# Macaron feed-forward layers of a decoder trunk: gate and up sums with the tokens stationary and 512 weight columns moving

## The chip, the cores and the metric

One Trainium2 chip, one of its NeuronCores. The metric is the device time of one execution of the whole program, in microseconds. The kernel before takes 970.08 us, the median of three runs (969.25 to 970.21).

## What is computed

Two layers of a decoder over 256 tokens with 1024 features, all in f32. Each layer is a half-weighted SwiGLU, a token mixer (short convolution and sliding-window attention in layer 0, causal block attention in layer 1), cross-attention to a memory of 256 rows, and a second half-weighted SwiGLU. A last RMSNorm follows. Cut to what the change touches:

```python
def rmsnorm(x, g):
    return x * lax.rsqrt(jnp.mean(x * x, axis=-1, keepdims=True) + EPS) * g

def swiglu(x, w_gate, w_up, w_down):          # 1024 -> 2816 -> 1024
    return (jax.nn.silu(x @ w_gate) * (x @ w_up)) @ w_down

for l in range(2):
    x = x + 0.5 * swiglu(rmsnorm(x, ffn1_norm[l]), ...)
    x = x + mixer(rmsnorm(x, mix_norm[l]))
    x = x + memory_cross_attention(rmsnorm(x, xa_norm[l]), ...)
    x = x + 0.5 * swiglu(rmsnorm(x, ffn2_norm[l]), ...)
return rmsnorm(x, final_norm)
```

So there are four feed-forward blocks (FFNs) in a run, each with 22 x 8 weight tiles of 128 x 128 for the gate, as many for up, and as many for down.

## The kernel before

**Layout.** The stream `x` lies with features on the partitions: 8 tiles (KT) of 128 features x 256 tokens. A matmul therefore has a weight tile as the stationary operand (loaded by LDWEIGHTS) and the tokens as the moving one, and its output has the output features on the partitions. The 22 (FT) hidden tiles `h[f]` come out in the layout that the down product needs.

**Precision.** Each f32 operand is split in two fp32r parts, hi and lo, and a product is hi*hi + hi*lo + lo*hi. `mm` (L389) does it with two matmuls for one weight tile: w-hi against 512 columns (x-hi and x-lo side by side, L392) and w-lo against the 256 of x-hi (L393). The bank then holds two halves, which `join` (L401) adds: a ScalarE copy (L402) and a VectorE add (L403). `mm_narrow` (L395) does it with three matmuls of 256 columns (L397 to L399) into one half. `group_tok` (L437, used by `v_group` in layer 1) is the third form: tokens stationary, four weight tiles (512 columns) moving, three matmuls for each half of the tokens (L449 to L451).

**Weights.** `Stream` reads all weights from DRAM in the order of use: chunks of 16 tiles (1 MB) through SP's queue, four `raw` buffers. A block is 8 tiles; ScalarE makes its hi part (L127) and VectorE its lo part (L128), into five `whi`/`wlo` buffers. `take` (L155) asks for the tile or the four tiles of a step and has blocks up to four ahead split; `fill` and `flush` write the splits that are due into the program at the places where they are called. The very first 32 tiles come with x in eight smaller loads of their own (`load_first`).

**Norm.** The gain goes into the tiles of x (`normed_tile`, L313). 1/rms of a token is left out and multiplied in later. `norm_scale` (L341) makes it: sums over features turned on TensorE (L353, or L355 for the first FFN), `rcol` on GpSimd (L360; a value for each token on the partitions), and with `wide` it is spread on TensorE (L366) and copied (L368) to `rbc`, where it lies along the free axis.

**An FFN** (`ffn`, L497). `gate_up` (L512) makes one f tile of gate or up: eight `mm`, then `join`. `evac` (L530) then multiplies the gate by `rbc` (L532), takes silu (L533), multiplies by up (L535) and splits into `h[f]` (L465, L466). The first FFN starts with `gates` (L501): the first four gate tiles together, in the order in which the first loads land. `down` (L540) makes one of the eight output tiles from all 22 `h`; its sum is joined, scaled by 0.5 and `rbc` (L549) and added to x (`add_to_x`, L459), and the next norm's tile is made at once. The last FFN ends in `down_tok` (L555), with tokens on the output partitions; there `to_tokens` (L482) turns x with VectorE's 32 x 32 transposes (L489) and DMAs through DRAM (L492, L494).

**Order.** `Order.run` writes fillers (matmul parts with their cost) and timed tasks out in one program order; the tile framework then orders each engine's instructions by its own simulated timeline, apart from those that are pinned. Each engine runs its list in order. PSUM has 4 banks `acc`, 2 `sc`, 2 `tr`.

## Time and profile before

| what | us |
|---|---|
| median of three runs | 970.08 (969.25 to 970.21) |
| span of the profiled execution, first to last instruction | 966.6 |
| gate and up of the FFN that begins at 312.68 (352 tiles) | 115.72 |
| down of the FFN that begins at 428.40 (176 tiles) | 57.80 |
| VectorE and ScalarE busy in that gate and up stage | 96.31 and 75.59 |
| VectorE and ScalarE busy in that down stage | 41.64 and 31.48 |

The times of the runs and the profile are of separate executions. The profiled one has no time of its own beside its span; what lies around the span is about 3.5 us if it ran like the median (970.08 less 966.6). The stage rows come from the view of the profile that sums busy time by stretch. Durations of matmuls overlap, since they are pipelined: what one costs is the distance from its start to the next one's start, which the view in order of time shows.

### The profile page before, as it was taken

How to read it: one execution, taken by the hardware profiler on the slowest of the kernel's cores; microseconds unless marked ns; L12 is line 12 of the kernel's file. 1: busy time of each engine (PE TensorE's matmuls, PEld its weight loads, DVE VectorE, ACT ScalarE, POOL GpSimd, SP SyncE). 2: the span in 40 equal slices, each digit the busy share in tenths (PEclk: the TensorE clock that was granted, in tenths of full speed). 3: DMA queues.
4: the chain of work that ended last, by engine and by line, in shares of the span. 5: the costliest groups of instructions: out<-in, count | busy, mean ns of one | idle time of the engine just before them, and what ended most of it. 6: DMA issues, size and time to landing. Idle time of an engine off the chain costs nothing.

```text
span 966.6 us, 17028 instructions
## 1 busy us (share of the span) xinstructions
PE 958.3 (99%) x6606; PEld 902.1 (93%) x6606; DVE 757.1 (78%) x1350; ACT 614.4 (64%) x1144; POOL 56.0 (6%) x95
## 2 busy tenths in 40 slices
PE   9999999999999999999999999999999999999997
PEld 9999999999999999999999999999999999999896
DVE  6979767898878888876778778677878789878663
ACT  7767655697658766665556666556786677666541
POOL 0410000001000000000000000000000003400011
PEclk9999999999999999999999999999999999999999
DMA  9797556455535655656556565565645356775531
GB/s 371 284 342 269 199 193 217 168 187 201 186 133 208 228 187 206 208 189 213 194 199 204 194 213 188 204 208 184 222 144 192 120 175 239 240 259 183 212 131 44
DMA packets 29922, 196.74 MB, mean 204 GB/s; under 512 B 3848, under 2 KB 4872, under 8 KB 7184
## 3 DMA queue, kind: packets, MB, share of 16 engines
q1 hardware_dynamic: 27072, 187.44, 55.0%
q0 software_dynamic: 2192, 7.37, 2.2%
q8 instruction: 52, 0.85, 0.3%
q10 hardware_dynamic: 576, 0.83, 0.2%
q14 instruction: 30, 0.25, 0.1%
HBM read 193.51 MB, written 5.27 MB: 206 GB/s over the span
## 4 chain that ended last, share of the span: by engine, by line
PE 99%; DMA 0%; DVE 0%; POOLq 0%; ACT 0%; SPq 0%; issue 0%; DVEq 0%
PE acc L392 41%; PE acc L393 20%; PE acc L397 8%; PE acc L399 8%; PE acc L398 8%; PE acc L581 1%; PE acc L580 1%; PE acc L579 1%; PE acc L923 1%; PE acc L922 1%; PE acc L921 1%; PE sc L579 0%; PE sc L581 0%; PE sc L580 0%; DMA raw<-in_w 0%; PE tr L756 0%
## 5 line engine op out<-in xcount | busy, mean ns | idle before, releaser
L127 ACT ACTIVATE whi<-raw 128x1024 fp32r<-128x1024 f32 (+2 forms) x377 | 369.5, 986 | 269.7 <-PE acc L392 131.9
L128 DVE TENSOR_TENSOR wlo<-raw,whi 128x1024 fp32r<-128x1024 f32 (+2 forms) x377 | 427.0, 1136 | 143.4 <-ACT whi L127 140.2
L392 PE MATMUL acc<-x,whi 128*128 128x512 f32 x1344 | 441.3, 383 | 0.0
L393 PE MATMUL acc<-x,wlo 128*128 128x256 f32 x1344 | 365.5, 273 | 0.0
L392 PEld LDWEIGHTS acc<-x,whi 128*128 128x128 f32 x1344 | 253.7, 189 | 34.8
L393 PEld LDWEIGHTS acc<-x,wlo 128*128 128x128 f32 x1344 | 258.0, 192 | 0.3
L392 PE MATMUL acc<-h,whi 128*128 128x512 f32 x462 | 151.3, 382 | 0.0
L393 PE MATMUL acc<-h,wlo 128*128 128x256 f32 x462 | 125.4, 273 | 0.0
L392 PEld LDWEIGHTS acc<-h,whi 128*128 128x128 f32 x462 | 87.1, 189 | 12.1
L397 PE MATMUL acc<-x,whi 128*128 128x256 f32 x352 | 95.5, 279 | 1.4 <-ACT whi L127 1.4
L399 PE MATMUL acc<-x,wlo 128*128 128x256 f32 x352 | 95.9, 278 | 0.0
L398 PE MATMUL acc<-x,whi 128*128 128x256 f32 x352 | 95.7, 277 | 0.0
L393 PEld LDWEIGHTS acc<-h,wlo 128*128 128x128 f32 x462 | 88.7, 192 | 0.2
L399 PE MATMUL acc<-h,wlo 128*128 128x256 f32 x322 | 87.7, 275 | 0.0
L398 PE MATMUL acc<-h,whi 128*128 128x256 f32 x322 | 87.7, 275 | 0.0
L397 PE MATMUL acc<-h,whi 128*128 128x256 f32 x322 | 86.5, 277 | 0.0
L403 DVE TENSOR_TENSOR w<-acc,w 128x256 f32<-128x256 f32 x189 | 78.7, 417 | 3.8 <-ACT w L402 3.5
L402 ACT ACTIVATE w<-acc 128x256 f32<-128x256 f32 x189 | 69.9, 370 | 8.3 <-PE acc L393 8.3
L397 PEld LDWEIGHTS acc<-x,whi 128*128 128x128 f32 x352 | 66.4, 192 | 1.8 <-ACT whi L127 1.6
L398 PEld LDWEIGHTS acc<-x,whi 128*128 128x128 f32 x352 | 66.8, 192 | 0.2
L399 PEld LDWEIGHTS acc<-x,wlo 128*128 128x128 f32 x352 | 66.7, 192 | 0.2
L398 PEld LDWEIGHTS acc<-h,whi 128*128 128x128 f32 x322 | 61.7, 192 | 0.1
(213 smaller groups left out, 1192.2 us busy)
## 6 DMA issues: line engine op xcount, KB each, us to landing
raw<-in_w SPq DMA_DIRECT2D x171, 1024.0 KB, 4.9
dists<-line POOLq DMA_DIRECT2D x2, 1536.0 KB, 13.3
raw<-in_memT SPq DMA_DIRECT2D x3, 1024.0 KB, 4.9
raw<-in_w SPq DMA_DIRECT2D x6, 384.0 KB, 6.8
bias<-dists POOLq DMA_DIRECT2D x2, 1024.0 KB, 11.1
x<-in_xT SPq DMA_DIRECT2D x1, 1024.0 KB, 7.5
tok<-q POOLq DMA_DIRECT2D x32, 32.0 KB, 3.5
bias<-tok POOLq DMA_DIRECT2D x1, 1024.0 KB, 8.1
```

The lines of the kernel that those rows point to most:

```text
L127: for ins in (self.nc.scalar.activation(hi[:, at], src, AF.Copy), self.nc.vector.tensor_tensor(lo[:, at], src, hi[:, at].bitcast(F32), op= ...
L128: self.nc.vector.tensor_tensor(lo[:, at], src, hi[:, at].bitcast(F32), op=ALU.subtract)):
L392: nc.tensor.matmul(ps, w[0], x2.both, start=start, stop=False)
L393: nc.tensor.matmul(ps[:, :S], w[1], x2.high, start=False, stop=stop)
L397: nc.tensor.matmul(ps[:, :S], w[0], x2.high, start=start, stop=False)
L398: nc.tensor.matmul(ps[:, :S], w[0], x2.low, start=False, stop=False)
L399: nc.tensor.matmul(ps[:, :S], w[1], x2.high, start=False, stop=stop)
L402: nc.scalar.activation(halves(out), unpaired(ps[:, S:]), AF.Copy)
L403: nc.vector.tensor_tensor(halves(out), unpaired(ps[:, :S]), halves(out), op=ALU.add)
L579: nc.tensor.matmul(ps, hh, wh, start=f == 0, stop=False)
L580: nc.tensor.matmul(ps, hh, wl, start=False, stop=False)
L581: nc.tensor.matmul(ps, hl, wh, start=False, stop=f == FT - 1)
```

## The change

Gate and up are computed with the tokens stationary. `rows_of` makes a row group: for each of the 8 feature tiles k it takes four weight tiles at once and runs, for each half u of the tokens, three matmuls with 512 weight columns moving into that half's bank; four f tiles of gate, then the same four of up. The last two f tiles (22 = 5 x 4 + 2) share one group of two gate and two up tiles (`both`). There is no sum of halves to join, and since tokens now lie on the partitions of the bank, 1/rms is a factor for each partition: ScalarE takes silu straight from the bank with `rcol` as its scale, and VectorE multiplies the up bank by `rcol` and by that result. `h` so made has tokens on the partitions; `turned_back` brings it into the layout that down needs, with VectorE's 32 x 32 transposes, one DMA to DRAM and four back, and the split into hi and lo reads what came back. Groups of four tiles use GpSimd's DMA queue, the last two tiles ScalarE's; two buffers (`v`, `k2`) take turns. `down` adds both halves of its bank to x, each with the factor 0.5. `downs` writes the first two output tiles with the first 20 `h`, then both with the last two, then the other six. `gates`, `evac`, `gate_up` and, in the FFNs, the spread 1/rms are gone; `make_bias` is told to wait for `rcol` instead of `rbc`.

```diff
--- before.py
+++ after.py
@@ -152,7 +152,7 @@
         while self.due or self.part:
             self.fill()
-    def take(self, name, layer, row, col, n=1, rows=1):
+    def take(self, name, layer, row, col, n=1, rows=1, other=None):
@@ -160,6 +160,7 @@
         for k in range(n):
             at = k % 2 * P
             self.order.append((name, layer, row, col + k * P, 1) if n == 1 else
+                              ((name, other)[k // 2], layer, row, col + at, 1) if other else
                               (name, layer, row, col + 2 * at + k // 2, 2) if rows == 1 else
                               (name, layer, row + at, col + k // 2, 2))
         b, o = divmod(i, BLK)
@@ -496,69 +497,111 @@
     def ffn(which, layer, n, nxt, first=False, last=False):
         h = [None] * FT
-        cur = {}
-
-        def gates():
...
+        gate, up = f"{which}_w_gate", f"{which}_w_up"
+        def turned_back(f0, s, c):
+            t = act.tile([P, 8 * c * 32], F32, name=("v", "k2")[f0 // 4 % 2], bufs=1)
+            to = t.rearrange("p (b u c i) -> p u c b i", b=4, u=2, c=c)
+            for u in range(2):
+                nc.vector.transpose(to[:, u], s[u].rearrange("p (c b j) -> p c b j", c=c, b=4))
+            queue = nc.gpsimd if c == 4 else nc.scalar
+            d = dram.tile([P, 8 * c * 32], F32, name="turn", bufs=2)
+            queue.dma_start(d, t)
+            for b in range(4):
+                queue.dma_start(t[32 * b:32 * b + 32].rearrange("j (a x) -> j a x", a=4),
+                                d.rearrange("(a j) (b x) -> b j a x", a=4, b=4)[b])
+            back = t.rearrange("p (a u c i) -> p c u a i", a=4, u=2, c=c)
+            for i in range(c):
+                h[f0 + i] = x2 = h_tile()
+                hi, lo = (m.rearrange("p u (a i) -> p u a i", a=4) for m in (x2.hi, x2.lo))
+                nc.scalar.activation(hi, back[:, i], AF.Copy)
+                nc.vector.tensor_tensor(lo, back[:, i], hi.bitcast(F32), op=ALU.subtract)
+        def rows_of(name, c, bank, evac, other=None):
+            ps = []
+            def part(ks):
+                def go():
+                    if ks[0] == 0:
+                        ps.extend(bank() for _ in range(2))
+                    for k in ks:
+                        wh, wl = (paired(w) for w in ws.take(name, layer, k * P, c, 4, other=other))
+                        for u in range(2):
+                            xh, xl = (n.x[k].v[:, u, m] for m in range(2))
+                            nc.tensor.matmul(ps[u], xh, wh, start=k == 0, stop=False)
+                            nc.tensor.matmul(ps[u], xh, wl, start=False, stop=False)
+                            nc.tensor.matmul(ps[u], xl, wh, start=False, stop=k == KT - 1)
+                    ws.flush()
+                    if ks[-1] == KT - 1:
+                        when_scaled(n, lambda: evac(ps))
+                return always, go, len(ks) * 1300
+            return [part(range(k, k + 2)) for k in range(0, KT, 2)]
+        def hidden(f0):
+            state = {}
+            def r(u):
+                return n.rcol[:, u:u + 1]
+            def gated(ps):
+                state["s"] = [w2() for _ in range(2)]
+                for u in range(2):
+                    nc.scalar.activation(state["s"][u], ps[u], AF.Silu, scale=r(u))
+            def product(ps):
+                for u, t in enumerate(state["s"]):
+                    nc.vector.scalar_tensor_tensor(t, ps[u], r(u), t, op0=ALU.mult, op1=ALU.mult)
+                turned_back(f0, state["s"], 4)
+            def both(ps):
+                ts = [w2()[:, :S] for _ in range(2)]
+                for u, t in enumerate(ts):
+                    g, v = ps[u].rearrange("p (a b) -> p b a", b=2)[:, 0], ps[u].rearrange("p (a b) -> p b a", b=2)[:, 1]
+                    nc.scalar.activation(t, g, AF.Silu, scale=r(u))
+                    nc.vector.scalar_tensor_tensor(t, v, r(u), t, op0=ALU.mult, op1=ALU.mult)
+                turned_back(f0, ts, 2)
+            if f0 + 4 > FT:
+                return rows_of(gate, f0 * P, acc_tile, both, up)
+            return (rows_of(gate, f0 * P, sc_tile if f0 // 4 % 2 else acc_tile, gated) +
+                    rows_of(up, f0 * P, acc_tile, product))
+        def down(j, ks, cell):
             def go():
                 if ks[0] == 0:
...
+                    cell.append(acc_tile())
+                ps = cell[0]
+                ws.fine = j == KT - 1
                 for k in ks:
...
                     w = ws.take(f"{which}_w_down", layer, k * P, j * P)
                     (mm_narrow if ws.fine else mm)(ps, w, h[k], k == 0, k == FT - 1)
...
+                if ks[-1] == FT - 1:
+                    for part in (ps[:, :S],) if ws.fine else (ps[:, :S], ps[:, S:]):
+                        nc.vector.scalar_tensor_tensor(halves(x[:, j]), unpaired(part), 0.5, halves(x[:, j]),
+                                                       op0=ALU.mult, op1=ALU.add)
+                    normed_tile(nxt, j, x[:, j], x)
                 ws.flush()
...
+            return always, go, len(ks) * 327
+        def downs():
+            cells = [[] for _ in range(KT)]
+            early = range(FT // 4 * 4)
+            late = range(FT // 4 * 4, FT)
+            return ([down(j, early, cells[j]) for j in range(2)] + [down(j, late, cells[j]) for j in range(2)] +
+                    [down(j, range(FT), cells[j]) for j in range(2, KT)])
         def down_tok():
             late = 2 * (ws.BUFS - 1)
-            half_r = act.tile([P, 2], F32, name="half_r", bufs=1)
-            pe.after(30000, lambda: nc.vector.tensor_scalar(half_r, n.rcol, 0.5, None, op0=ALU.mult), 0)
             pss, got, mean = {}, {}, [EPS, EPS]
             def part(fs, *regions):
@@ -587,7 +630,7 @@
             def evac_tok(u, at, ps):
                 y = xtok[:, u, at]
-                nc.vector.scalar_tensor_tensor(y, ps, half_r[:, u:u + 1], y, op0=ALU.mult, op1=ALU.add)
+                nc.vector.scalar_tensor_tensor(y, ps, 0.5, y, op0=ALU.mult, op1=ALU.add)
                 ms = act.tile([P, 1], F32, name="mean", bufs=4)
                 junk = w2()[:, :at.stop - at.start]
                 nc.vector.tensor_tensor_reduce(junk, y, y, 1.0 / D, mean[u], ALU.mult, ALU.add, ms)
@@ -614,18 +657,15 @@
         if first:
             for k in range(KT):
                 pe.after(12000 + 1800 * (k // 2), lambda k=k: squares(n, k, x), 0)
-        norm_scale(n, 18900 if first else 2300, unpin=True, turn=not first)
...
+        norm_scale(n, 18900 if first else 2300, unpin=True, turn=not first, wide=False)
         if last:
             xtok = act.tile([P, 2, D], F32, name="bias", bufs=1)
             gfin = act.tile([P, D], F32, name="kT", bufs=1)
             src = a["final_norm"]
             nc.sync.dma_start(gfin, bass.AP(tensor=src.tensor, offset=src.offset, ap=[[0, P], [1, D]]))
             when_scaled(n, lambda: pe.after(6000, lambda: to_tokens(xtok), 0))
...
+        ups = [f for f0 in range(0, FT, 4) for f in hidden(f0)]
+        pe.run(ups + (down_tok() if last else downs()))
     def small(name):
@@ -1104,7 +1144,7 @@
     def biases():
         nc.vector.tensor_scalar(nsinks, vecs[:, VCOL["sinks"]:VCOL["sinks"] + 8], -1.0, None, op0=ALU.mult)
-        make_bias(n.rbc)
+        make_bias(n.rcol)
         early["bias"] = load_bias(0)
     mn = new_normed("mem_norm", "h", FT, keep=True)
```

More of the change, by code (lines that the diff above doesn't have):

```diff
@@ L513, in go @@
+        def down(j, ks, cell):
             def go():
                 if ks[0] == 0:
-                    cur[f, part] = acc_tile()
-                ps = cur[f, part]
-                w = f"{which}_w_{'up' if part else 'gate'}"
-                narrow = first and f < SIDE
+                    cell.append(acc_tile())
+                ps = cell[0]
+                ws.fine = j == KT - 1
                 for k in ks:
-                    (mm_narrow if narrow else mm)(ps, ws.take(w, layer, k * P, f * P), n.x[k], k == 0, k == KT - 1)
@@ L616, in ffn @@
                 pe.after(12000 + 1800 * (k // 2), lambda k=k: squares(n, k, x), 0)
-        norm_scale(n, 18900 if first else 2300, unpin=True, turn=not first)
-        parts = (range(4), range(4, KT))
-        ups = [(always, gates, FIRST * 327)] if first else []
-        ups += [gate_up(f, part, ks) for f in range(FT) for part in range(2) for ks in parts
-                if not (first and part == 0 and f < SIDE)]
+        norm_scale(n, 18900 if first else 2300, unpin=True, turn=not first, wide=False)
         if last:
@@ L627, in ffn @@
             when_scaled(n, lambda: pe.after(6000, lambda: to_tokens(xtok), 0))
-        pe.run(ups + (down_tok() if last else [down(j) for j in range(KT)]))
+        ups = [f for f0 in range(0, FT, 4) for f in hidden(f0)]
+        pe.run(ups + (down_tok() if last else downs()))
     def small(name):
```

34 lines of the change are left out of this document (removed).

## The prediction

> **What bounds the kernel now.** I read the page first: span, busy shares, slices, the chain that ended last.
>
> ```profile
> span 966.6 us, 17028 instructions
> PE 958.3 (99%) x6606; PEld 902.1 (93%) x6606; DVE 757.1 (78%) x1350; ACT 614.4 (64%) x1144; POOL 56.0 (6%) x95
> PEclk9999999999999999999999999999999999999999
> PE 99%; DMA 0%; DVE 0%; POOLq 0%; ACT 0%; SPq 0%; issue 0%; DVEq 0%
> ```
>
> The reader is to see one engine in charge. TensorE (PE) is 99% of the chain, and its granted clock is full in all slices. VectorE's 78% and ScalarE's 64% lie beside it. So two things alone move the end: the time that a matmul takes until the next can start, and any new place where PE waits. Busy time can't tell the first, since matmuls overlap; the view in order of time can. First the pair that `mm` issues for one weight tile, in a gate and up stage:
>
> ```profile
> 379.93 0.38 PE L392 MATMUL acc<-x,whi 128*128 128x512 f32 x1
> ...
> 400.89 0.38 PE L392 MATMUL acc<-x,whi 128*128 128x512 f32 x1
> ```
>
> From the first row to the last lie 64 pairs without a gap: 20.96 us / 64 = 327.5 ns for a tile. Now whole stages, in the view of busy time by stretch (stretch, sum, then busy time and instructions of PE, PEld, DVE, ACT, POOL, then clock, DMA share, GB/s). The second row is `v_group` of layer 1, the form that the change brings:
>
> ```profile
> 312.68:428.40 115.72, 115.72 (x711) 106.53 (x709) 96.31 (x163) 75.59 (x139) 1.61 (x1) 1.00 0.59 208
> 670.88:681.23 10.35, 10.35 (x50) 9.08 (x49) 10.08 (x19) 8.68 (x17) 0.00 (x0) 1.00 0.64 222
> 5.98:27.97 21.99, 21.99 (x195) 21.95 (x196) 18.48 (x29) 18.84 (x34) 1.30 (x2) 1.00 1.02 416
> ```
>
> `v_group` is 8 steps of k with 6 matmuls: 48 in 10.35 us (the count has two that reach in), 215.6 ns each, for 32 tiles. That is 323.4 ns a tile. Both forms stream 768 columns for a tile, so the gain can't be large. It is 4.1 ns a tile, because four 512-wide and four 256-wide matmuls become six of 512. VectorE was 97% and ScalarE 84% busy in that stretch, so the step holds beside full neighbours.
>
> Over N columns the Trainium skill ("TensorE: Matmul & The Clock Gate", section Back-to-back issue gap) gives a start-to-start of N / 2.4 + 2.5 ns. By it the wide step is 215.8 ns, and the trace agrees (215.6); but the pair would be 325.0 ns where the trace has 327.5. By the page a tile would gain 1.3 ns, by the rows 4.1, and the measurement decides.
>
> **The change part by part.** Everything is counted against the profiled span of 966.6 us and carried over to the median: 970.08 less 966.6 is 3.5 us around the span, which no part of the change touches.
>
> *Three full FFNs.* Now 115.72 us. After: 352 x 323.4 ns = 113.84. Two of the four small transposes stay, those of the sums. Those of the spread 1/rms go:
>
> ```profile
> L366 PE MATMUL tr<-ident,rcol x12: 272/272/273, 30.6 to 803.2; 128*128 128x128 f32 x12
> ```
>
> 115.72 less 352 x 327.5 ns (115.28) leaves 0.44 us for four, 0.11 each. So 113.84 + 0.22 = 114.06, a gain of 1.66 us each, 5.0 in three.
>
> *The first FFN.* 288 of its tiles run as pairs: 288 x 4.1 ns = 1.18, plus the spread 0.22, makes 1.4 us. Its first 64 run with three 256-wide matmuls and take 21.99 us from 5.98 on (third row above). About 0.4 of that is the four short matmuls of the sums, which stay; 64 x 323.4 ns + 0.4 = 21.1, a gain of 0.9. Against it stands the start:
>
> ```profile
> 5.41 0.52 ACT L127 ACTIVATE whi<-raw 128x384 fp32r<-128x384 f32 x1 [1.41 <-DMA raw<-in_w]
> 5.96 0.56 DVE L128 TENSOR_TENSOR wlo<-raw,whi 128x384 fp32r<-128x384 f32 x1 [1.45 <-ACT whi L127]
> 5.98 0.38 PE L397 MATMUL acc<-x,whi 128*128 128x256 f32 x1 [1.43 <-ACT whi L127]
> ```
>
> A wide matmul needs all four tiles, so it can't start before 5.98 (one narrow matmul did), and its lo part is there at 6.52. Between nothing and 0.32 us is lost there; with the early matmul I take 0.3. First FFN together: 1.4 + 0.9 - 0.3 = 2.0 us.
>
> *Down, `down_tok`, attention, end.* Same matmuls. The two halves of a bank are now added by two VectorE instructions in place of join, scale and add; PE waits for none of these today. I count nothing.
>
> **PE gains 5.0 + 2.0 = 7.0 us**, if nothing new makes it wait.
>
> *Load on the other engines.* For four f tiles VectorE had 8 joins (417 ns), 4 + 4 multiplies (417, 424) and 4 lo parts (415); ScalarE 8 copies (370), 4 silus (408), 4 hi parts (406). After: VectorE two 512-wide multiplies from the bank, two transposes, 4 lo parts; ScalarE two 512-wide silus and 4 hi parts.
>
> ```profile
> L403 DVE TENSOR_TENSOR w<-acc,w 128x256 f32<-128x256 f32 x189 | 78.7, 417 | 3.8 <-ACT w L402 3.5
> L402 ACT ACTIVATE w<-acc 128x256 f32<-128x256 f32 x189 | 69.9, 370 | 8.3 <-PE acc L393 8.3
> L535 DVE TENSOR_TENSOR w<-w,w 128x256 f32<-128x256 f32 x88 | 36.7, 424 | 8.3 <-DVE w L403 0.9 <-ACT w L533 0.8
> L465 ACT ACTIVATE h<-w 128x256 fp32r<-128x256 f32 x96 | 38.1, 406 | 2.2 <-DVE w L535 1.0 <-DVE w L887 1.0
> L466 DVE TENSOR_TENSOR h<-w,h 128x256 fp32r<-128x256 f32 x96 | 39.2, 415 | 0.0
> L489 DVE STREAM_TRANSPOSE q<-x 128x512 f32<-128x512 f32 x4 | 2.7, 695 | 0.0
> 955.21 0.75 DVE L590 SCALAR_TENSOR_TENSOR bias<-sc,half_r,bias 128x512 f32<-128x512 f32 x1 [5.50 <-PE sc L581]
> ```
>
> VectorE falls from 8.4 to 2 x 0.75 + 2 x 0.70 + 1.7 = 4.6 us for 20.7 us of PE, ScalarE from 6.2 to about 3. It frees time, but not time on the path.
>
> *The way of h through DRAM is the one new wait that can reach PE.* Its places are the first `h` of the fifth group (f 16 to 19) and f 20, 21. Earlier groups have 40 us and more until down begins; the last FFN's `down_tok` uses one f in 1.3 us, so f 16 has 31 us. Rows for the transfers, of the DMA view and of GpSimd's order of time:
>
> ```profile
> raw<-in_w SPq DMA_DIRECT2D x171, 1024.0 KB, 4.9
> tok<-q POOLq DMA_DIRECT2D x32, 32.0 KB, 3.5
> bias<-tok POOLq DMA_DIRECT2D x1, 1024.0 KB, 8.1
> out<-bias ACTq DMA_DIRECT2D x2, 192.0 KB, 2.1
> L492 POOL DMA_DIRECT2D tok<-q x32: 582/582/624, 813.9 to 839.9; - x32
> 50.52 1.09 POOL L869 DMA_DIRECT2D dists<-line  x2 [3.64 <-DMA line<-kT]
> DMA to landing us min/median/max: 1.8/3.5/5.4
> ```
>
> *Cover of f 16*: the last row group, 48 x 0.2156 = 10.35 us, and 16 tiles of down, 16 x 0.3275 = 5.24: 15.6 us. *Chain*: two multiplies and two transposes, 2.9, with part of a weight split ahead 3.5; the round trip R; then ScalarE's hi part, VectorE's lo part and parts of two splits, 1.9. It is in time for R up to 10.2. R is a 512 KB write, three more issues (0.58 each, 1.75) and the landing of the last 128 KB read. From below two landings at 1.8 (the shortest of the 32): 5.4. From above two at 8.1 (1 MB on this queue): 17.95. I take 4.9 for the write and 3.5 for the read, the rows nearest in size and queue: 10.15. So f 16 is just in time, and f 17 to 19 follow at 0.41 us against 0.33 needed. **0.3 us lost in each of three FFNs, 1.0 us together.** From below it is nothing, from above 7.8 each.
>
> *Cover of f 20*: 40 tiles of down, 13.1 us. Chain: 2.2 of arithmetic, a 256 KB write on ScalarE's queue (2.1 for 192 KB; 2.5), the reads 3.5, 1.9 at the end: 10.1. In time, but ScalarE issues these DMAs itself: each read waits for the write in ScalarE's own list, and behind it stand hi parts of weights and of f 16 to 19. PE has four blocks (10.5 us) of split weights ahead, so 3 us of that cost nothing.
>
> By the Trainium skill ("DMA: Bandwidth & Descriptors", section Anatomy of one DMA) a transfer through GpSimd's queue costs 2.0 us plus its bytes at 436 GB/s, an estimate of 3.2 us for the write and 2.3 for a read. Then R would be 7.3 and nothing would be late. The trace speaks against it: 32 KB took 3.5 us in the median, and PE gains 7.0 instead of 6.0.
>
> **Sum**: 970.08 - 7.0 + 1.0 = **964.1 us**.
>
> **The rivals.**
>
> *Late turns that take back the gain.* PE waits in the first output tile of down. If R is 12.0 to 13.1, 1.8 to 2.9 us are lost in each of three FFNs, 5.1 to 8.7, and the kernel ends within 0.2% of before. For: another kind of transfer on this queue took 8.1. Against: weight loads of 1 MB land in 4.9 beside the same traffic.
>
> *Late turns that make it slower.* The same place, with R over 13.1: PE stands 2.9 us or more in each of three downs. At R = 15 it is 4.8 each, 14.4 together: 977.5 us. Above 13.1 ScalarE is also held at the hi parts of f 16, the turn of f 20 starts late, and a second wait follows. For: all five DMAs of a group wait in GpSimd's list one after another, and a 24 KB write alone held it 3.64 us. Against: GpSimd is idle in these stretches.
>
> *The wide form doesn't run at 215.6 in an FFN.* If the 4.1 ns came from traffic in the stage and not from the alternation of widths, only the spread (4 x 0.22) and part of the first tiles remain, about 1.5 us, less 1.0 for the turns: 969.6. Against: `v_group` had VectorE at 97%. Halfway, with a pair that an undisturbed stage would run 2.5 ns faster than 327.5, a tile gains 1.6 ns and the run ends at 970.08 - (1344 x 1.6 ns = 2.2) - 1.5 + 1.0 = 967.8. The clock page's formula in the Trainium skill is of this kind (1.3 ns a tile); the trace's 64 pairs without a gap speak against it.
>
> **How the numbers follow.** A measurement of this kernel can tell about 0.2%, 1.9 us, from no change: faster is below 968.1, slower above 972.0. The forecast with turns late by less than 1.8 us in an FFN (963.1 to 968.1): 0.79. Late turns within 0.2%: 0.09. Wide form not faster: 0.03, within; halfway: 0.01, faster. Late turns, slower: 0.08. So faster 0.80, same 0.12, slower 0.08. The lowest sum is 963.1 with no turn late; half a microsecond below it allows for the spread of the runs. At the top the range takes the forecast's own bound and the lower part of late turns: 962.6 to 969.0. It leaves out R above 12.2, about 0.15.
>
> **What would show it.** Right: the stretch of 352 gate and up tiles takes about 114.1 us, and VectorE and ScalarE are less busy in it; the chain is still 99% PE; the first output tile of down shows gaps of some tenths of a microsecond, released by VectorE's lo part of `h`. Wrong: PE idle by microseconds before a matmul that reads `h`, or in gate and up behind a weight split (ScalarE or VectorE held by the DMA in their list); a step of the wide matmuls above 216 ns; a first row group that ends later than 27.

## The result and the profile after

The kernel after takes 978.16 us, the median of seven runs (972.51 to 980.36). The kernel before took 970.08 beside it (969.22 to 970.30). The ratio is 1.0078, with a 95% interval of 1.0057 to 1.0100: about 8 us slower, where 964.1 was predicted. The profiled run took 979.09 us. From its page:

```profile
span 977.3 us, 15067 instructions
PE 957.3 (98%) x5830; PEld 877.2 (90%) x5830; DVE 683.2 (70%) x1077; ACT 556.4 (57%) x903; POOL 106.8 (11%) x195
PEclk9999979999999999999999999999999999999999
PE 86%; DMA 8%; issue 2%; POOL 2%; ACT 1%; DVE 1%; POOLq 0%; SPq 0%; DVEq 0%; ACTq 0%
```

VectorE and ScalarE are freer than before, as meant. But DMA now has 8% of the chain that ended last, where it had none, and in the sixth slice the granted clock is not full. The view of busy time by stretch (stretch, length, busy time and instructions of PE, PEld, DVE, ACT, POOL, then clock, DMA share, GB/s) puts it in its place. Gate and up of the first three FFNs stand here, each with the seven outputs of its down that run as pairs:

```profile
5.89:122.45 116.56, 115.78 (x539) 100.72 (x539) 79.85 (x105) 67.24 (x96) 23.06 (x53) 1.00 0.90 323
122.45:183.97 61.52, 53.41 (x308) 48.49 (x307) 38.56 (x53) 26.61 (x37) 2.79 (x5) 0.92 0.62 209
323.15:437.33 114.18, 114.18 (x532) 99.97 (x531) 77.60 (x94) 62.06 (x80) 14.05 (x24) 1.00 0.73 248
437.33:491.44 54.11, 52.28 (x309) 47.55 (x308) 35.42 (x50) 26.53 (x37) 1.37 (x3) 0.97 0.63 216
498.91:613.10 114.19, 114.19 (x533) 99.97 (x531) 73.31 (x87) 58.95 (x75) 14.51 (x26) 1.00 0.75 247
613.10:663.42 50.32, 50.32 (x308) 46.26 (x307) 35.04 (x50) 26.58 (x37) 0.00 (x0) 1.00 0.64 218
```

Gate and up take 114.18 us where they took 115.72: the gain is there. Down takes 50.32 in the third FFN, 3.8 more in the second and 11.2 more in the first. TensorE's order of time in the first down (start, duration, line, operation; in brackets the idle time before and what ended it):

```profile
130.85 0.27 PE L394 MATMUL acc<-h,wlo 128*128 128x256 f32 x1
139.23 0.79 PE L393 MATMUL acc<-h,whi 128*128 128x512 f32 x1 [8.11 <-DVE h L519]
...
140.03 0.63 PE L393 MATMUL acc<-h,whi 128*128 128x512 f32 x1
...
144.51 0.63 PE L393 MATMUL acc<-h,whi 128*128 128x512 f32 x1
```

TensorE stands 8.1 us for `h[16]`. Then, from 140.03 to 144.51, seven pairs take 0.64 us each instead of 0.3275: the granted clock is 0.50 from 134.82 to 145.06 (rows in the last section), which costs 2.9 us more. 8.1 and 2.9 are the 11.2 of this stage but for 0.2. Why was that `h` so late? ScalarE's order of time at the hi parts of turned tiles (L518), in the first FFN and, last row, in the third:

```profile
82.96 1.33 ACT L518 ACTIVATE h<-k 128x256 fp32r<-128x256 f32 x4 [7.70 <-DMA k<-turn]
96.56 1.34 ACT L518 ACTIVATE h<-v 128x256 fp32r<-128x256 f32 x4 [5.12 <-DMA v<-turn]
113.79 1.34 ACT L518 ACTIVATE h<-k 128x256 fp32r<-128x256 f32 x4 [9.65 <-DMA k<-turn]
138.31 0.42 ACT L518 ACTIVATE h<-v 128x256 fp32r<-128x256 f32 x1 [9.47 <-DMA v<-turn]
...
534.16 1.34 ACT L518 ACTIVATE h<-v 128x256 fp32r<-128x256 f32 x4
```

In the first FFN ScalarE stood 5 to 10 us not only at f 16 but at f 4, 8 and 12, 13 to 41 us before down's first matmul on them. Behind those copies in its list stand splits of weights. In the third FFN it hardly waited. The DMA view of a stretch (transfer, queue, count, size, median us from issue to landing) for the first FFN, 30 to 140 us:

```profile
raw<-in_w SPq DMA_DIRECT2D x19, 1024.0 KB, 8.7
turn<-v POOLq DMA_DIRECT2D x3, 512.0 KB, 6.4
v<-turn POOLq DMA_DIRECT2D x12, 128.0 KB, 7.5
```

and for the third, 520 to 630 us:

```profile
raw<-in_w SPq DMA_DIRECT2D x21, 1024.0 KB, 5.5
turn<-v POOLq DMA_DIRECT2D x3, 512.0 KB, 3.2
v<-turn POOLq DMA_DIRECT2D x12, 128.0 KB, 4.8
```

The round trip R, from the issue of the write to the landing of the last read, took 15.1, 30.3, 22.3, 17.4 and 15.7 us for the five groups of the first FFN, 10.1, 10.0, 9.3, 13.7 and 14.1 in the second, 10.2 to 10.7 in the third. The longest stood in GpSimd's queue behind the bias table of `make_bias`:

```profile
50.10 1.09 POOL L909 DMA_DIRECT2D dists<-line  x2 [6.54 <-DMA line<-kT]
...
52.54 0.56 POOL L510 DMA_DIRECT2D turn<-k  x1
```

### The profile page after: what moved, and what is told of

Its sections match the earlier page's. It is cut to its first block, busy times and chain, and to the rows that moved or that the text cites. A ratio compares the mean times of both kernels' runs of the same rounds, so it can differ in the third digit from the quotient of the medians.

```text
span 977.3 us, 15067 instructions
## 1 busy us (share of the span) xinstructions
PE 957.3 (98%) x5830; PEld 877.2 (90%) x5830; DVE 683.2 (70%) x1077; ACT 556.4 (57%) x903; POOL 106.8 (11%) x195
## 4 chain that ended last, share of the span: by engine, by line
PE 86%; DMA 8%; issue 2%; POOL 2%; ACT 1%; DVE 1%; POOLq 0%; SPq 0%; DVEq 0%; ACTq 0%
PE acc L533 10%; PE acc L534 10%; PE acc L535 10%; PE acc L393 10%; PE acc L398 7%; PE acc L400 7%; PE acc L399 7%; PE acc L394 5%; DMA v<-turn 3%; PE sc L535 2%; PE sc L534 2%; PE sc L533 2%; DMA turn<-k 2%; PE acc L623 1%; PE acc L624 1%
## 5 line engine op out<-in xcount | busy, mean ns | idle before, releaser
L534 PE MATMUL acc<-wlo,x 128*128 128x512 f32 x576 | 218.5, 379 | 0.8 <-DVE wlo L128 0.8
L535 PE MATMUL acc<-whi,x 128*128 128x512 f32 x576 | 218.1, 379 | 0.0
L533 PE MATMUL acc<-whi,x 128*128 128x512 f32 x576 | 215.5, 380 | 1.4 <-ACT whi L127 1.4
L393 PE MATMUL acc<-h,whi 128*128 128x512 f32 x462 | 156.0, 390 | 9.9 <-DVE h L519 9.9
L533 PEld LDWEIGHTS acc<-whi,x 128*128 128x128 f32 x576 | 108.8, 189 | 17.1 <-ACT whi L127 1.9
L534 PEld LDWEIGHTS acc<-wlo,x 128*128 128x128 f32 x576 | 108.9, 189 | 16.6 <-DVE wlo L128 1.4
L535 PEld LDWEIGHTS acc<-whi,x 128*128 128x128 f32 x576 | 108.9, 189 | 15.3
L393 PEld LDWEIGHTS acc<-h,whi 128*128 128x128 f32 x462 | 89.2, 194 | 23.5 <-DVE h L519 10.5
L394 PEld LDWEIGHTS acc<-h,wlo 128*128 128x128 f32 x462 | 90.7, 196 | 0.2
L400 PE MATMUL acc<-x,wlo 128*128 128x256 f32 x304 | 84.1, 278 | 0.0
L399 PE MATMUL acc<-x,whi 128*128 128x256 f32 x304 | 83.8, 277 | 0.0
L398 PE MATMUL acc<-x,whi 128*128 128x256 f32 x304 | 83.3, 278 | 0.0
L399 PEld LDWEIGHTS acc<-h,whi 128*128 128x128 f32 x322 | 61.7, 192 | 0.1
L400 PEld LDWEIGHTS acc<-h,wlo 128*128 128x128 f32 x322 | 61.7, 192 | 0.1
L398 PEld LDWEIGHTS acc<-h,whi 128*128 128x128 f32 x322 | 60.6, 192 | 0.4 <-DVE x L461 0.2
L399 PEld LDWEIGHTS acc<-x,whi 128*128 128x128 f32 x304 | 58.2, 192 | 0.2
## 6 DMA issues: line engine op xcount, KB each, us to landing
dists<-line POOLq DMA_DIRECT2D x2, 1536.0 KB, 14.2
```

The lines of the kernel that those rows point to most:

```text
L393: nc.tensor.matmul(ps, w[0], x2.both, start=start, stop=False)
L394: nc.tensor.matmul(ps[:, :S], w[1], x2.high, start=False, stop=stop)
L398: nc.tensor.matmul(ps[:, :S], w[0], x2.high, start=start, stop=False)
L399: nc.tensor.matmul(ps[:, :S], w[0], x2.low, start=False, stop=False)
L400: nc.tensor.matmul(ps[:, :S], w[1], x2.high, start=False, stop=stop)
L533: nc.tensor.matmul(ps[u], xh, wh, start=k == 0, stop=False)
```

## The experiments

The ratios are against runs of the kernel before on the same chip. "Down 1" is the stretch of the first FFN's down as above, in us, from the profiled run alone (50.3 where nothing waits). Each kernel is the changed one with the edit named. Where a median below is set against the 978.16 us of the changed kernel, the two come from different chips; the kernel before had medians of 968.49 to 970.08 there, so such a difference is good to some 1.6 us. The ratios don't have this fault.

| kernel | median (range) us | ratio (95%) | down 1 |
|---|---|---|---|
| e1, no DMAs in the turn | 963.06 (961.72 to 963.31) | 0.9938 (0.9923 to 0.9953) | 50.3 |
| e2, turn's DMAs unread | 965.49 (965.31 to 965.68) | 0.9964 (0.9951 to 0.9977) | 50.3 |
| e3, longer cover | 968.61 (964.98 to 971.53) | 0.9998 (0.9985 to 1.0011) | 53.0 |
| e5, weight loads halved | 967.52 (965.84 to 970.43) | 0.9990 (0.9978 to 1.0002) | 51.6 |
| e8, table issued by SyncE | 975.58 (972.75 to 977.53) | 1.0058 (1.0042 to 1.0075) | 59.6 |
| e9, table late | 976.50 (975.86 to 977.72) | 1.0074 (1.0057 to 1.0091) | 59.3 |
| e13, table and memory late | 966.15 (963.01 to 978.87) | 0.9986 (0.9959 to 1.0012) | 51.3 |
| e11, early hi and lo on GpSimd | 966.53 (963.05 to 974.39) | 0.9983 (0.9957 to 1.0009) | 52.0 |
| e12, e11 and e3 | 964.61 (964.34 to 966.33) | 0.9958 (0.9945 to 0.9972) | 51.3 |
| e14, e12 and e13 | 964.42 (963.40 to 970.78) | 0.9943 (0.9929 to 0.9956) | 56.2 |
| e15, 3 MB more in FFN 3 | 976.36 (973.95 to 978.94) | 1.0078 (1.0053 to 1.0103) | 58.8 |
| e17, copies later in the list | 966.00 (962.51 to 974.70) | 0.9980 (0.9958 to 1.0002) | 50.3 |
| e18, e17 and e3 | 964.05 (962.53 to 972.88) | 0.9961 (0.9942 to 0.9979) | 50.3 |

**Is it the turn at all? (e1, e2)**

```diff
...
-            queue.dma_start(d, t)
-            for b in range(4):
-                queue.dma_start(t[32 * b:32 * b + 32]..., d...[b])
```

> Leaves out the five DMAs of each turn: the split into hi and lo reads the tile as VectorE's transposes left it, so h is turned only inside blocks of 32. Theory A (PE loses only where it waits for an h whose way through DRAM is late, directly or because ScalarE stands in its list at that read): all waits of PE for h go, and the sum of the prediction comes out, 963.1 us within 1.0. Rival C (the new kernel loses in more places than the turn: the wide form, the silu from the bank, the longer tail): 966 or more. Rival B (GpSimd's software queue is slow by itself) says the same as A here.

Time by stretch, the first FFN and its down:

```profile
5.47:122.60 117.13, 117.13 (x538) 102.34 (x539) 85.13 (x111) 70.39 (x100) 14.55 (x33) 1.00 0.79 296
122.60:172.93 50.33, 50.33 (x309) 46.24 (x307) 34.01 (x46) 25.59 (x33) 0.00 (x0) 1.00 0.59 203
```

963.06 us, against 963.1 predicted for no turn late; no loss elsewhere (C falls). The second FFN takes 114.18 and 50.33 us in the same view. The 15 us between this and the changed kernel (14.5 when each is counted against the kernel before beside it) are the turn's.

e2 keeps every DMA but reads into a tile that nobody uses (`t2` in place of `t`; the last FFN is left as it is).

> All DMAs of a turn go on, with the same sizes and queues, but those coming back land in another tile that nobody reads; the split reads the tile that went out (in the last FFN they land in the tile itself as before). So the traffic stays and the wait of ScalarE, VectorE and PE for it goes. Theory A (waiting is what costs): 963 to 964.5 us. Rival D (the traffic itself costs, because it delays the weight loads until PE runs out of split weights): 968 or more, with PE idle before matmuls that wait for wlo or whi.

965.49 us and no wait in the first three downs, though R in its first FFN was 14 to 35 us. The time lies 1 us above what theory A allowed and 2.4 above e1, so the traffic (D), or the last FFN's turns, which are still read there, cost that much. The rest, some 12 us, is the price of waiting for the turns. One more thing showed here: its weight loads were issued 3.8 to 6.1 us apart from 75 us to the end of that FFN. In the changed kernel the starts ran 84.6, 86.8, 90.1, 92.4, then 100.1, 102.5, 105.4, then none until 118.6. So the bunches need the waiting: the same transfers without it don't bunch.

**Cover, and the weight loads ahead of the reads (e3, e5)**

```diff
-            early = range(FT // 4 * 4)           # first two outputs: 20 tiles of h first
+            early = range(FT // 4 * 4 - 4)       # first three outputs: 16 tiles first
```

> Down begins with three output tiles over the first 16 h (before: two over the first 20), then the rest of these three. The fifth group's h is first read 10.35 + 48 x 0.3275 = 26.1 us after its sums end instead of 15.6, the last two tiles' later still. Theory A: a round trip of 14 to 16 us, as seen in the profile, then fits, no PE wait for h is left in down, 963.5 to 966 us; a wait of about 1 us for split weights in gate and up of the first FFN may stay. If turns were late by much more than the profile shows, or if PE loses elsewhere, over 968.

Cover alone gives back 9.5 us of the median, but not the 963.5 to 966 expected, and nothing is won over the kernel before. Even in the profiled run, the fastest of the ten (964.98), ScalarE stood 6.2, 3.5, 8.1 and 7.1 us at its copies all the same, and the splits behind them came late (TensorE waits of 1 us).

> Weight loads carry half their bytes: each chunk brings its first 8 tiles only and both blocks are split from these, so half of the weights are left out of the computation; all other work is as in the changed kernel. Theory A (the turn's packets wait behind weight loads that were issued before them on the same 16 engines): the slowest read of a turn lands in 6 us or less instead of 10.2, and no PE wait for h is left: 963 to 965 us. Rival B (GpSimd's queue is slow by itself): the reads still take 8 to 10 us and the time stays at 972 or more.

(The edit loads the first half of each chunk, so half of the weights are left out.) 967.52 us fits neither expectation. The reads landed after 3.0 us in the median instead of 4.6, so they do wait for weight loads, and R fell to about 8.4 in the later FFNs. But in the first the turn of f 4 still took 14 us for its write alone and ScalarE stood 4.6 to 9.1 us: smaller loads alone don't end the waiting there. B, a GpSimd queue that is slow by itself, doesn't fit the reads that became faster.

**Does it begin at the bias table? (e6, e8, e9, e13)** The first try only moved the call in the program:

```diff
-    pe.after(30000, biases, 0)
+    pe.after(135000, biases, 0)
```

> The changed kernel with one thing moved: the bias table of the even mixer is built, spread by the two 1536 KB DMAs and loaded back behind the turns of the first FFN instead of in their midst (due at 135 us of the planner's time instead of 30). Nothing is left out. In the changed kernel's trace those two DMAs are issued at 50.1 and 50.7 us on GpSimd's queue, and the write of the turn of h tiles 4 to 7, issued 2 us behind them, lands only 19 us later. Theory A (the 8.1 us stall of TensorE starts there: ScalarE stands at that group's hi copies, the splits behind them bunch, raw buffers come free in bunches, and the loads in bursts delay the next turns): the turns of the first FFN take about 10 us as the later ones do, ScalarE stands under 1 us ahead of its hi copies, TensorE waits 0 to 2 us at 131 us, the down stage takes 50 to 54 us instead of 61.5, and the time falls by 7 to 12 us to 966 to 971. Rival (the first FFN is late by its own group period of 21 us and its first weight loads, whatever the table does): turns of 14 us and more and a stall of 4 us and more stay, and the time is 974 or above.

975.07 us (974.44 to 977.93). It told nothing: GpSimd's list is ordered by the simulated timeline, and the table's DMAs still started at 51.5 us. (Together with e3's cover the same edit gave 967.44 (e7, 963.09 to 973.19), as cover alone, where 962.5 to 965.5 was expected.) e8 issues the two DMAs from SyncE, the load of the bias tile staying where it was in the list:

> The changed kernel with the two 1536 KB DMAs of the table issued by SyncE instead of GpSimd, at about the same time (50 to 60 us), and the load of the bias tile behind the first FFN's turns. Nothing is left out; the same bytes move beside the turns. If the turn was late because its write stood behind these two in one queue, the write of tiles 4 to 7 lands in 5 us or less, ScalarE stands under 2 us, and the time is that of the kernel with the table moved away, within 2 us. If the traffic itself does it, or the weight loads that now stand behind the two on SyncE's queue, splits and turns are late still: turns of 14 us and more, TensorE waits of 4 us and more in the first FFN, and a time of 974 and above.

The write of f 4 now took 12.0 us instead of 19, so its place in the queue was part of it, but the later turns took 16 to 23 us as before and the time did not move. e9 makes the table wait for data (with the 135000 of e6):

```diff
+                if first and f0 + i == 19:
+                    early["after"] = hi.bitcast(F32)[:, 0, 0]
-        make_bias(n.rcol)
+        make_bias(early["after"])
```

> The changed kernel with the build of the bias table (its copies, the two 1536 KB DMAs and the load of the bias tile) made to wait for h tile 19 of the first FFN, so that on GpSimd's queue it stands behind all the turns of that FFN; the earlier try moved it only in the program and left the queue's order as it was. Nothing is left out. Theory A (the first FFN's stall starts at the table's DMAs): the turns of the first FFN take 10 to 12 us, ScalarE stands under 1 us ahead of the hi copies of f0 to f11, TensorE waits 0 to 2 us at 131 us, and the time falls to 964 to 970. Rival (the first FFN's turns are late by the group's own period, its loads and ScalarE's list, whatever the table does): turns of 14 us and more and a TensorE wait of 4 us and more stay, time 974 or above.

The table was gone to 142 us, and our theory fell: 976.50. ScalarE's hi parts, in order of time:

```profile
50.96 1.34 ACT L518 ACTIVATE h<-v 128x256 fp32r<-128x256 f32 x4 [1.83 <-DMA v<-turn]
67.65 1.32 ACT L518 ACTIVATE h<-k 128x256 fp32r<-128x256 f32 x4
92.67 1.33 ACT L518 ACTIVATE h<-v 128x256 fp32r<-128x256 f32 x4 [9.88 <-DMA v<-turn]
116.93 1.34 ACT L518 ACTIVATE h<-k 128x256 fp32r<-128x256 f32 x4 [11.31 <-DMA k<-turn]
```

The turn of f 4 held nobody. Then came the squares of the memory (`mem_scale`, 65 to 73 us on ScalarE and VectorE), and from f 8 on ScalarE stood 10 and 11 us. Time by stretch in between shows what standing does:

```profile
95.00:105.00 10.00, 9.22 (x43) 7.92 (x44) 10.00 (x12) 7.54 (x9) 0.56 (x1) 1.00 0.57 191
105.00:120.00 15.00, 13.38 (x61) 10.86 (x59) 3.73 (x7) 3.69 (x8) 2.92 (x5) 1.00 0.69 223
120.00:125.00 5.00, 4.22 (x20) 3.70 (x20) 5.00 (x7) 4.34 (x5) 0.00 (x0) 1.00 0.40 133
```

VectorE is busy all of 10 us, then 3.73 of 15, then all of 5. The splits run back to back and free the `raw` buffers together; three loads then start 2.4 us apart, and the next turn's reads, issued behind them, take nearly twice as long as in the third FFN. From the DMA view, 100 to 112 us:

```profile
raw<-in_w SPq DMA_DIRECT2D x3, 1024.0 KB, 8.8
k<-turn POOLq DMA_DIRECT2D x4, 128.0 KB, 8.9
```

The DMA engines are busy only 0.4 to 0.7 of the stretches above. But from 100 to 112 us, while these reads are on their way, most slices of the view show them 90% busy and more: what is to spare on the average isn't there when the reads come. This suggested theory L: a late turn holds ScalarE and VectorE, that bunches the loads, and the bunch makes the next turn late. By the Trainium skill ("DMA: Bandwidth & Descriptors", section Queues, rings and completion order) a DMA engine goes round its queues packet by packet, so that three loads on SyncE's queue should not hold up GpSimd's more than one does. These rows don't bear that out: 8.9 us behind three loads, 4.8 in the third FFN, where loads start 5.2 us apart.

e13 moves the memory's load and squares behind the turns as well (`pe.after(60000, mem_scale, 0)` to 136000).

> The changed kernel with both one-off jobs of the first FFN moved behind its turns: the bias table as before, and now the load and the squares of the memory (a 1 MB load among the weight loads, 5 us of work on ScalarE and VectorE). Nothing is left out. With the table alone moved, the turns of f0 and f4 left ScalarE no idle time worth naming (1.8 and 0.0 us), the memory's squares came at 65 to 73 us, and from there the loads ran three in a row 2 to 2.4 us apart with pauses of 13 to 15 us, and ScalarE stood 8 to 11 us at every later turn. Theory L (a loop that keeps itself up: a turn whose reads stand behind two or three loads holds ScalarE and VectorE at its copies, the splits behind them then free the raw buffers together, and the loads that follow stand ahead of the next turn; any one-off job can start it, and without one the loads keep their 5.2 us apart): loads 5 us apart all through the first FFN, turns of 9 to 11 us, ScalarE idle under 1 us ahead of its hi copies, no TensorE stall over 1 us, time 963 to 967. Rival (the first FFN is late by its start, with its first eight loads at full rate, or by something not seen): the loop is there again by 80 us, a stall of 4 us and more, time 973 or above.

Six of ten runs took 963.0 to 966.8 us, four 971.9 to 978.9. Without the one-off jobs the loss is mostly gone, but not always, and theory L's "under 1 us" was missed: in the profiled run (965.53) ScalarE still stood 3.2, 4.6 and 4.6 us at f 8, 12 and 16. So these jobs make it worse, but they aren't the whole cause.

**Taking the wait out of the lists (e11, e12, e14)** For f 0 to 15 of the first three FFNs:

```diff
+                if f0 < 16 and not last:
+                    nc.gpsimd.tensor_copy(hi, back[:, i])
+                    nc.gpsimd.tensor_tensor(lo, back[:, i], hi.bitcast(F32), op=ALU.subtract)
+                    continue
```

> The changed kernel with the hi copies and lo subtractions of the turned h tiles 0 to 15 of the first three FFNs put on GpSimd, so that neither ScalarE nor VectorE can stand at an early turn; tiles 16 to 21 and the table stay as they were. Nothing is left out. If ScalarE's standing at early turns is what makes the turn of f16 late (splits bunch, raw buffers come free in bunches, the loads in bursts stand ahead of the turn's packets): the stall at 131 us falls from 8.1 to 0 to 3 us and the time to 965 to 971. If the traffic of the table and of the loads does it without ScalarE: the turn of f16 still takes 14 to 16 us, the stall stays at 5 us and more, and the time is 974 or above.

966.53: most of the loss is regained with ScalarE and VectorE out of the early turns, though R was 15 to 31 us in the first FFN. Single runs reach up to 974.39.

> The two edits that each gave back most of the loss, together: hi and lo of h tiles 0 to 15 of the first three FFNs on GpSimd (no early turn can hold ScalarE or VectorE), and three outputs over the first 16 h tiles ahead of the rest (more cover for the turn of f16). Nothing is left out. Theory L: the loop cannot form before f16, and a turn of f16 of up to 15 us is covered: no TensorE stall over 0.5 us in the FFNs, 962.5 to 965.5 with little scatter, ratio to the kernel before 0.993 to 0.997. Rival (GpSimd's slower copies are themselves late, or the waits sit elsewhere): 966 and above, as with either edit alone.

964.61, 0.4% faster than the kernel before, and steady over five runs.

> The kernel with the early hi and lo copies on GpSimd and the longer cover (964.61 before), with the bias table and the memory's squares moved behind the first FFN's turns as well. Nothing is left out. In the former's profiled run two TensorE waits were left in the first FFN: 1.8 us at 104.9 and 0.9 us at 140. Theory L (the one-off jobs are what still disturbs the loads and turns there): both go, turns of the first FFN take 9 to 13 us, and the time falls to 962.3 to 964.3, as low as without any turn (963.06). Rival (the first FFN's loads lag from the start, or the moved jobs now delay the mixer's bias): 964.5 or above.

964.42, no better. In its slowest run (970.78, the profiled one) the waiting had only moved house. GpSimd's order of time:

```profile
115.66 2.49 POOL L519 CAST h<-k 128x256 fp32r<-128x256 f32 x4 [9.14 <-DMA k<-turn]
118.13 4.85 POOL L520 TENSOR_TENSOR h<-k,h 128x256 fp32r<-128x256 f32 x4
122.93 0.58 POOL L510 DMA_DIRECT2D turn<-v  x1
```

GpSimd stands 9.1 us at the copies of f 12, and the write of f 16, whose data were there at 115.7, is issued behind them at 122.9.

**A disturbance put where there was none (e15)** Six 512 KB writes of the turned tile into the table's DRAM tile, on GpSimd's queue between the turns of f 0 and f 4 of the third FFN.

> The changed kernel with 3 MB more to write, in the third FFN, whose turns all took 10 to 12 us and cost TensorE nothing: six 512 KB DMAs of the turned tile of f0 to f3 into the table's DRAM tile, which nobody reads any more, on GpSimd's queue behind the turn of f0, so between it and the turn of f4. The rest is as before, and nothing is left out. Theory L (a loop that keeps itself up once started): the turn of f4 takes 14 us and more, ScalarE stands there, and the turns of f8, f12 and f16, which come 20 to 60 us after the last of the added bytes has landed, still take 13 us and more with ScalarE idle 4 to 10 us ahead of their copies; loads come in bunches; TensorE waits 3 to 8 us at the end of that FFN's sums, and the kernel is 3 to 9 us slower than the changed kernel (978.16): 981 to 987. Rival (each disturbance passes by itself, and the first FFN is late for reasons of its own): f8 or f12 is back at 9 to 11 us, no TensorE wait over 1 us in the third FFN, and the time is 976 to 980.

As quick as the changed kernel; theory L's number was missed. ScalarE at the turns of f 4 and 8:

```profile
557.24 1.33 ACT L518 ACTIVATE h<-k 128x256 fp32r<-128x256 f32 x4 [0.34 <-DMA k<-turn]
569.75 1.32 ACT L518 ACTIVATE h<-v 128x256 fp32r<-128x256 f32 x4
```

The turn of f 4 did take 18.3 us, but the tile framework, whose timeline has the added writes in it, had put these copies further down ScalarE's list, 18 us after the turn's write in place of 10. So ScalarE waited 0.34 us, and the next turn took 9.9. One slow turn that nobody waits for didn't start the loop. (ScalarE did stand 2.5 us at f 12 and at f 16, where the changed kernel has 0.4 and none; those turns took 12.7 and 11.9 us, and TensorE waited for none.) (With 1 MB instead of 3, e16, no turn of that FFN was late; 976.80, inside the 976 to 980 expected, with runs from 970.46 to 989.85.)

**The place in the list alone (e17, e18)** That gave the cleanest test. The hi copies of f 0 to 15 get a column of ones as their scale, made from the next group's product, so that they, and the lo parts after them, can't stand in the lists before it:

```diff
...
+            if held:
+                one = act.tile([P, 1], F32, name="one", bufs=2)
+                nc.vector.tensor_scalar(one, s[1][:, :1], 0.0, 1.0, op0=ALU.mult, op1=ALU.add)
+                held.pop()(one)
+            if f0 < 16 and not last:
+                held.append(copies)
...
```

> The changed kernel with one place in ScalarE's and VectorE's lists changed: in the first three FFNs the hi and lo copies of the turned tiles 0 to 15 wait for the product of the next group (through a column of ones made from it), and so stand six splits of 1024 columns behind that group's gate silus instead of two. Counted at 2.6 us a split, ScalarE comes to them some 20.7 us after the turn's write is issued instead of 10.3. Engines, bytes, queues and the turn of f16 to f19 are as they were; the one-off jobs too. Nothing is left out. Theory L as it now stands (a turn costs nothing until ScalarE comes to its copies before it has landed; from then on the splits behind bunch, the loads bunch, and the next turn is late too): with turns of 10 to 20 us nobody stands, loads stay 5.2 us apart in the first FFN, the turns of f12 and f16 there take 9 to 12 us, TensorE waits under 1.5 us, the time is 963 to 966 with a scatter of 1 to 2 us. Rival (a lasting cause in the first FFN makes its turns late): the turn of f16 takes 14 us and more all the same, TensorE waits 4 us and more, 972 and above.

966.00 us, 12 less than the changed kernel (10.6 when each is counted against the kernel before beside it), with the same engines, bytes and queues, apart from the small column. Time by stretch, first FFN and its down:

```profile
5.62:123.80 118.18, 117.20 (x539) 102.19 (x540) 84.02 (x111) 69.72 (x96) 25.99 (x58) 1.00 0.94 335
123.80:174.12 50.32, 50.32 (x309) 46.24 (x307) 35.17 (x50) 26.82 (x37) 0.00 (x0) 1.00 0.67 220
```

and ScalarE's hi parts in it (L522 here):

```profile
83.40 1.70 ACT L522 ACTIVATE h<-k,one 128x256 fp32r<-128x256 f32 x4 [6.82 <-DMA k<-turn]
97.56 1.71 ACT L522 ACTIVATE h<-v,one 128x256 fp32r<-128x256 f32 x4 [2.85 <-DMA v<-turn]
117.19 1.69 ACT L522 ACTIVATE h<-k,one 128x256 fp32r<-128x256 f32 x4
127.93 1.34 ACT L522 ACTIVATE h<-v 128x256 fp32r<-128x256 f32 x4 [0.31 <-DMA v<-turn]
```

The turn of f 4 took 29 us as ever, with table and memory in its way. But the wait dies out, 6.8, 2.9, 0, where it kept up or grew before; the turn of f 16 took 10.5 us instead of 15.7, and down lost nothing. At f 4 the edit moved nothing: ScalarE came 22 us after the write's issue (23 in the changed kernel) and stood. At f 12 it came after 20 us instead of 8. The loads bunch once, at 85.4, 87.6, 90.9 and 93.1, and from 98 on start 4 to 7 us apart. So in this run the jobs at the start do pass; there is no lasting cause. "Nobody stands" was missed, and the range of 962.5 to 974.7 is wider than forecast.

The second FFN, far from the one-off jobs, tells the same over all profiles. The turn of f 12 takes 11.5 to 14.8 us there in each kernel that has turns and whole weight loads. In seven of them (the changed kernel, e3, e6, e7, e8, e13, e16) ScalarE stood 3.0 to 4.3 us for it, and the turn of f 16 then took 12.6 to 14.2 us. In the other eight ScalarE stood 1.4 us at most, because nobody reads the turn (e2), the copies are on GpSimd (e11, e12, e14) or later in the list (e17, e18), or the turn was the quickest (e9 and e15, 11.5); their turn of f 16 took 9.1 to 10.3. This is the link from one late turn to the next.

> The same with the longer cover (three outputs over the first 16 tiles). Nothing is left out. Theory L: no wait of over 0.5 us is left ahead of any down stage; 962.5 to 964.5, as low as the kernel without trips (963.06), and below the 964.6 of the version with the copies on GpSimd. Rival: 965 and above.

964.05 us, the lowest median of a kernel that does the whole computation, though by the ratio no better than e12 and e14; its single runs reach from 962.53 to 972.88. The profiled run is this slowest one, and its down lost nothing. What it lost stands in another in-order list, GpSimd's (last row: TensorE):

```profile
107.43 2.18 POOL L514 DMA_DIRECT2D k<-turn  x4 [9.15 <-DMA turn<-k]
109.62 0.74 POOL L361 TENSOR_TENSOR rcolm<-ms,mhalf 128x2 f32<-128x2 f32 x1
110.41 0.43 PE L367 MATMUL tr<-ident,rcolm 128*128 128x128 f32 x2 [2.83 <-POOL rcolm L361]
```

GpSimd stood 9.15 us for the write of f 12 before it could issue the reads, and behind them stands the memory's 1/rms, for which TensorE waited 2.83 us. The clock was at half from 111.59 to 115.00, and again from 920.55 to 923.96, after waits of 0.86 and 0.78 us for weight splits in the last FFN. These waits and the two slow stretches make some 8 of the 10 us above the fastest run. In e11's profiled run (971.10) the wait for the memory's 1/rms was 4.4 us.

## Why the prediction was wrong

**The step that failed** is the one sentence that freed the early groups: "Earlier groups have 40 us and more until down begins". Down does need them that late. ScalarE doesn't: their copies stand in its in-order list, two splits behind the next group's silus, with the weights of the next matmuls behind them. In the second and third FFN it comes to them 10 us after the turn's write is issued; in the first it came after 23, 17, 8 and 6 us (R less its wait, f 4 to f 16), against turns of 30 to 16. So every turn had a deadline, not the last one alone, and a ScalarE held at an early turn makes the later ones late. e17 changed the place of the copies alone and gave back 12 us (10.6 against the kernel before beside each); e2, where nobody waits, gave back 13 (12.1).

**R was sized right for an undisturbed stage, the cover and the chain were not.** 10.15 us was taken; the third FFN has 10.2 to 10.7. By the prediction's sum that should cost some tenths there, and it cost nothing, because 26 tiles of down ran ahead of the first matmul on f 16 (122.45 to 130.96 in the first FFN), not 16: a cover of 18.9 us, not 15.6. What was missing is that R depends on its surroundings: 14 to 30 us behind the table, the memory or bunched loads. And in the first FFN the write of f 16 was issued 10.4 us after its sums ended (112.1), not the 3.5 of the chain (3.9 in the third). VectorE, which makes its products and transposes, had stood at f 12 (second row: GpSimd, the write):

```profile
114.24 1.43 DVE L519 TENSOR_TENSOR h<-k,h 128x256 fp32r<-128x256 f32 x4 [8.84 <-ACT h L518]
122.50 0.59 POOL L510 DMA_DIRECT2D turn<-v  x1 [16.43 <-DVE v L507]
```

So of what made f 16 later than in the third FFN, 6.5 us are the late write and 5.5 the longer R. The estimate of 7.3 us by the Trainium skill ("DMA: Bandwidth & Descriptors", section Anatomy of one DMA) was met by no turn beside whole weight loads; the shortest took 8.8 (e9).

**The gain of TensorE was right.** 114.18 for a gate and up stage against 114.06: 1.54 us for each of three, not 1.66. Nothing lost in down, as said (50.33). The 2.0 us of the first FFN can be had but not always: from the first matmul to the first of down its stage took 117.20 before, 116.56 in the changed kernel, 117.13 in e1, 115.34 in e3 and 114.67 in e13. In e1 matmuls started 0.43 us apart until 9.5 us, the pace of the half clock, so that 12 started from 5.98 to 10 us where e13 has 20. When the clock rises differs from run to run, and no sum had it. In all, e1 against before is 0.62% or 6.0 us (4.6 to 7.5 by the interval) where 7.0 was predicted.

**The rival "late turns that make it slower"** is what came, at its very time (977.5 for R = 15), but in other parts: not 4.8 in each of three downs but 11.2, 3.8 and 0. That the time agrees is luck. "Above 13.1 ScalarE is also held" was written there as an effect of the last turn; it came first, three turns earlier. The second wait, at f 20, did not come: the first had covered it. And the half clock after a wait was in no sum: 2.9 and 1.8 us of the two downs. Two of the rivals' sums were added up wrongly: 1.8 us in three FFNs are 5.4, not 5.1, and the halfway case ends at 967.4, not 967.8. The forecast doesn't use them.

**Open**: what decides in a single run how much is lost. e13, e17 and e18 each have runs near 963 and runs above 972; of these slow ones only e18's was profiled, and it lost its time elsewhere. What makes the turn of f 12 slow in the second FFN was not tested. The memory's squares were not moved without the table.

## What to carry to other kernels

The deadline of a round trip through DRAM is not when the bounding engine needs the data, but when the first in-order engine comes to the instruction that reads them; look up what stands behind that instruction in its list. Put such an instruction as far down the list as its consumer allows, by a data dependence if the order is made by a scheduler, before you shorten the trip. The engine that issues the trip has such a list too: what stands behind the reads waits for the write. A turn that is just in time in one stage must be tried beside the one-off jobs of another.

## What was not expected of the hardware

After the 8.1 us wait TensorE ran at half clock for 5.8 us of unbroken work. A wait of 1.8 us in the second down also brought it, and only later: apart from the first pair matmuls ran at full pace from 447.84 to 448.8 and then at half until 452.2. Time by stretch, with the granted clock in the third number from the end:

```profile
134.82:145.06 10.24, 5.83 (x18) 5.00 (x19) 4.64 (x9) 5.01 (x9) 0.00 (x0) 0.50 0.35 111
448.84:452.26 3.42, 3.42 (x13) 2.94 (x12) 1.55 (x2) 2.64 (x5) 0.00 (x0) 0.50 0.23 59
```

The Trainium skill ("TensorE: Matmul & The Clock Gate", section What's actually happening) has the clock fall after an idle window of some 3.4 us; here less than 2 us were enough. Nor does the length of the wait alone decide: 1.6 us in e12 didn't bring it, and of two pairs of waits with one matmul between, the 0.9 and 0.8 us of e18 did and the 1.0 and 0.8 us of e3 didn't. In all these profiles a fall in mid-run lasted 3.4, 6.8 or 10.2 us. The two stalls here cost their own length and 2.9 and 1.8 us more.
